# Column sums of a LayerNorm on VectorE, and part of the weights' low parts by accumulating DMA transfers

## The chip, the core and the metric

One core of one Trainium2 chip. The metric is the device time of one execution, in microseconds (us); lower is better. A core has TensorE (matrix products, its results go to PSUM), VectorE, ScalarE, GpSimd (POOL) and SyncE (SP). In this kernel SP's queue issues the loads, POOL's queue the transfers that add to what is already in the on-chip memory (SBUF).

## The reference, cut to what matters

One encoder layer on 256 positions with 2048 channels, in float32. The part that bears on the change:

```python
z = jnp.einsum("bsd,de->bse", x, w_in[i]) + b_in[i]          # 2048 -> 3072
y_conv = conformer_conv(z[..., :s1], z[..., s1:s2], ...)     # 1024 channels
y_pool = multiscale_pool(z[..., s2:s3], ...)                 # 512 channels
y_four = fourier_mix(z[..., s3:], ...)                       # 512 channels
mixed = jnp.concatenate([y_conv, y_pool, y_four], axis=-1)
mix_out = jnp.einsum("bsm,md->bsd", mixed, w_out[i]) + b_out[i]
x = layer_norm(ALPHA * x + mix_out, ln1_g[i], ln1_b[i])

def conformer_conv(val, gate, w_dw, b_dw, ln_g, ln_b):
    u = val * jax.nn.sigmoid(gate)
    y = depthwise_conv(u, w_dw, width=31) + b_dw
    return jax.nn.silu(layer_norm(y, ln_g, ln_b))            # mean and variance over 1024 channels
```

After it come a gated feed-forward part, a per-layer embedding part and a second LayerNorm.

## The kernel before, in words

**Products in three passes.** Every large product of float32 numbers is made of three matmuls in a rounded format (float32r): each operand is split into a high part (the rounded number) and a low part (the rest), and `mm3` (lines 162 to 165) adds high times high, high times low and low times high into one PSUM tile. `split` (line 123) makes the two parts: ScalarE writes the high part by a cast (line 125), VectorE the low part by a subtraction (line 126).

**Weights.** `weights` (line 128) walks over a weight matrix in blocks of four rows of 128: a load of 1 MB on SP's queue into one of four `raw` buffers (line 121), then for each half of the block (two rows of 128, 1024 columns) a split into one `whi` and one `wlo` tile; there are four buffers of each. `pump` then issues some of the convolution's work that is pending. `project` (line 167) runs the matmuls of one 512-column block: for each of 16 rows of weights two position halves of three matmuls, so 12 matmuls for each half block. All instructions are written in program order and a planner then orders them for each engine by its own estimate of what is ready, earlier program order first; each engine and each queue works strictly in that planned order.

**The stage around the change.** The input projection runs in six column blocks: `glu(0)`, `glu(1)`, the pool block (column 4), `glu(2)`, `glu(3)`, the Fourier block (column 5). Each `glu` gives two of the eight 128-channel blocks of the convolution, whose 31 taps are shared between VectorE and ScalarE (`convolve`, lines 281 to 291); channels lie on partitions, so `mixc` is 128 partitions x 8 blocks x 256 positions. Between `glu(2)` and `glu(3)` the residual is loaded (line 379), scaled by ScalarE (line 381), and its bias is added by two accumulating transfers of 1 MB on POOL's queue (line 382). POOL's queue also carries the small bias rows (line 205). Then the output projection starts with the rows that belong to the pool and Fourier halves (`out_chunk`, line 427; its sums are added to the residual in line 431): two column chunks before the convolution's LayerNorm and two after it, in program order.

**The convolution's LayerNorm.** Channels lie on partitions and blocks, so the sum over channels of a position goes across partitions. `channel_mean` (line 444) does it by TensorE: for each of eight blocks and two position halves a matmul with the block as the stationary operand and one column of ones (of 1/1024) as the moving one, in plain float32 (line 449). `across` (line 454) brings the result back to all partitions: a diagonal matrix with the values (line 459), multiplied by ones (line 460). `column` (line 463) copies the mean's column out of PSUM. `squares` subtracts the mean (line 472) and squares on ScalarE (line 474). The reciprocal root (`rsqrt`, lines 68 to 85) is made by VectorE on one column per position half. Then each block is multiplied by it (line 480), goes through the swish on ScalarE (line 482) and is split. These parts feed the rest of the output projection (line 494).

Later stages use the same `split` and `mm3`. In the feed-forward part POOL's queue carries accumulating transfers of 1 MB (lines 617 and 629).

Of the kernel before, what the change touches and what calls it, by code (L numbers as in the profile page):

```python
# [9 lines left out]
F32 = mybir.dt.float32  # L10
F32R = mybir.dt.float32r
I32 = mybir.dt.int32
AF = mybir.ActivationFunctionType
ALU = mybir.AluOpType
PSUM = bass.MemoryType.PSUM

P = 128
D = 2048
S = 256
NT = S // P  # L20
# [4 lines left out]
NC = 512  # L25
ALPHA = float(2.0 ** 0.25)
EPS = 1e-5
KD = D // P
NCH = 8
POOL_WINDOWS = (2, 4, 8, 16)  # L30

PUMP = 1.3
# [35 lines left out]
def rsqrt(nc, pool, var, shape, tag):  # L68

    v = pool.tile(shape, F32, name="rs_v", tag=tag + "v")  # L70
    nc.vector.tensor_scalar(v, var, EPS, None, op0=ALU.add)
    y = pool.tile(shape, F32, name="rs_y", tag=tag + "y")
    nc.vector.tensor_scalar(
        y.bitcast(I32), v.bitcast(I32), -0.5, float(0x5F3759DF), op0=ALU.mult, op1=ALU.add
    )
    nc.vector.tensor_scalar(v, v, -0.5, None, op0=ALU.mult)
    a = pool.tile(shape, F32, name="rs_a", tag=tag + "a")
    for _ in range(3):
        if shape[1] == 1:
            nc.vector.tensor_scalar(a, y, v, y, op0=ALU.mult, op1=ALU.mult)  # L80
        else:
            nc.vector.tensor_tensor(a, y, y, op=ALU.mult)
            nc.vector.tensor_tensor(a, a, v, op=ALU.mult)
        last = nc.vector.scalar_tensor_tensor(y, in0=a, scalar=1.5, in1=y, op0=ALU.add, op1=ALU.mult)  # L84
    return y, last
# [3 lines left out]
def encoder_layer(ctx: ExitStack, tc, t):  # L89
    nc = tc.nc  # L90
# [7 lines left out]
    ptp = ctx.enter_context(tc.tile_pool(name="ptp", bufs=2, space=PSUM))  # L98

    ident = cpool.tile([P, P], F32, name="ident")  # L100
# [4 lines left out]
    def pump(budget):  # L105

        if hold[0] > 0:
            hold[0] -= 1
            return
        credit[0] += budget  # L110
        while pending and credit[0] > 0:
            cost = next(pending[0], None)
            if cost is None:
                pending.pop(0)
            else:
                credit[0] -= cost
        if not pending:
            credit[0] = 0.0
# [6 lines left out]
        nc.scalar.copy(hi, src)  # L125
        return nc.vector.tensor_tensor(lo, src, hi.bitcast(F32), op=ALU.subtract)  # L126

    def weights(dram, nk, spare=0, first=False):

        for u in range(0, nk, 4):
            n = min(4, nk - u)
            raw = wraw.tile([P, n * NC], F32, name="raw", tag="raw")
            small_steps = first and u == 0
            if not small_steps:
                m = n // 2 if first and u == 4 else n
                for h in range(0, n, m):
                    load(raw[:, h * NC : (h + m) * NC], dram[u // 4][:, h * NC : (h + m) * NC])  # L140
            if u >= nk - spare:
                th = apool.tile([P, 8, S], F32R, name="ahi", tag="ahi").rearrange("p a b -> p (a b)")
                tl = apool.tile([P, 8, S], F32R, name="alo", tag="alo").rearrange("p a b -> p (a b)")
            for h in range(0, n, 2):
                if u >= nk - spare:
                    hi, lo = (
                        x[:, h * NC : (h + 2) * NC].rearrange("p (k n) -> p k n", n=NC) for x in (th, tl)
                    )
                else:
                    hi = wsp.tile([P, 2, NC], F32R, name="whi", tag="whi")  # L150
                    lo = wsp.tile([P, 2, NC], F32R, name="wlo", tag="wlo")
                src = raw[:, h * NC : (h + 2) * NC].rearrange("p (k n) -> p k n", n=NC)
                if not small_steps:
                    split(src, hi, lo)
                    pump(PUMP)
                for k in range(2):
                    if small_steps:
                        load(src[:, k, :], dram[0][:, (h + k) * NC : (h + k + 1) * NC])
                        split(src[:, k, :], hi[:, k, :], lo[:, k, :])
                    yield u + h + k, hi[:, k, :], lo[:, k, :]  # L160
# [3 lines left out]
        nc.tensor.matmul(out, ahi, wlo, start=False, stop=False, **more)  # L164
        nc.tensor.matmul(out, alo, whi, start=False, stop=stop, **more)  # L165

    def project(dram, nk, act, bias=None, behind=0, spare=0, first=False, halves=False):

        ps = [pacc.tile([P, NC], F32, name="acc", tag="acc") for _ in range(NT)]
        if halves:
            ps.append(pacc.tile([P, NC], F32, name="acc", tag="acc"))

        def step(i, k, hi, lo, whi, wlo):
            c = slice(P, S) if i else slice(0, P)
            n = slice((i - 1) * S, i * S) if halves and i else slice(0, NC)
            mm3(  # L180
                ps[i][:, : n.stop - n.start], hi[:, c], lo[:, c], whi[:, n], wlo[:, n],
                k == 0, k == nk - 1 and bias is None,
            )

        late = []
        ahead = act(0)
        for k, whi, wlo in weights(dram, nk, spare, first):
            if k == LAG:
                while deferred:
                    deferred.pop(0)()  # L190
            ops = (k, *(act(k) if k else ahead), whi, wlo)
            step(0, *ops)
            if k >= nk - behind:
                late.append(ops)
            else:
                for i in range(1, len(ps)):
                    step(i, *ops)
        for i in range(1, len(ps)):
            for ops in late:
                step(i, *ops)  # L200
        if bias is not None:
            one2, bsh, bsl, pool = bias[0]
            brow = pool.tile([2, NC], F32R, name="brow", tag="brow", bufs=2)
            for i, part in enumerate((bsh, bsl)):
                nc.gpsimd.dma_start(
                    brow[i : i + 1, :].rearrange("o (a b) -> o a b", b=P), part[4 * bias[1] : 4 * bias[1] + 4, :]
                )
            for j in range(NT):
                nc.tensor.matmul(ps[j], one2, brow, start=False, stop=True)
        return ps  # L210
# [20 lines left out]
    with tc.tile_pool(name="conv", bufs=1) as conv:  # L231
        par = conv.tile([P, C_END], F32, name="par")
        col = lambda c: par[:, c : c + 1]
        ones = conv.tile([P, P], F32, name="ones")
        mixc = conv.tile([P, 8, S], F32, name="mixc")
# [15 lines left out]
        xhi, xlo, xact = act_tiles(2)  # L251
# [12 lines left out]
        y = [mixc[:, i, :] for i in range(NCH)]  # L264
# [28 lines left out]

        def glu(c, act):

            ps = project(t["w_in"][c], KD, act, first=c == 0)
            if c == 0:
                nc.sync.dma_start(ident, t["const"][:, K_ID : K_ID + P])
                nc.sync.dma_start(par, t["par"])
                nc.sync.dma_start(ones, t["const"][:, K_ONE : K_ONE + P])  # L300
            deferred.append(lambda: glu_end(c, ps))
            if c == 0:
                hold[0] = HOLD
# [37 lines left out]
        mix = [pfp.tile([P, 4, S], F32, name=f"mix{i}", tag="mix") for i in range(2)]  # L341


        ps = project(t["w_in"][4], KD, xact, bias=(biases, 4))
        with tc.issue_after(last_load[0].ins):
            nc.sync.dma_start(kst[:, K_MT - K_CH :], t["const"][:, K_MT:])

# [38 lines left out]
        glu(3, xact)  # L386


        ps = project(t["w_in"][5], KD, xact, bias=(biases, 5))

        def fourier_end(ps):
            zf = pfp.tile([P, NC], F32, name="zpf", tag="zpf", bufs=3)
# [50 lines left out]

        def channel_mean(src):

            out = [ptp.tile([P, NC], F32, name="tp", tag="tp")[:, 0:1] for _ in range(NT)]
            for i, x in enumerate(src):
                for j in range(NT):
                    nc.tensor.matmul(
                        out[j], x[:, j * P : (j + 1) * P], ones[:, 0:1], start=i == 0, stop=i == NCH - 1  # L450
                    )
            return out

        def across(v):

            out = ptp.tile([P, NC], F32, name="tp", tag="tp")
            for j in range(NT):
                diag = plep.tile([P, P], F32, name="diag", tag="diag", bufs=2)
                nc.vector.tensor_scalar(diag, ident, v[j], float(NCH * P), op0=ALU.mult, op1=ALU.mult)
                nc.tensor.matmul(out[:, j * P : (j + 1) * P], ones, diag, start=True, stop=True)  # L460
            return out[:, :S]

        def column(src):
            out = plep.tile([P, 1], F32, name="colv", tag="colv", bufs=4)
            nc.vector.tensor_copy(out, src)
            return out

        mean = across([column(m) for m in channel_mean(y)])

        def squares():  # L470
            for i in range(NCH):
                nc.vector.tensor_tensor(y[i], y[i], mean, op=ALU.subtract)
                sq = plep.tile([P, S], F32, name="sq", tag="sq", bufs=4)
                nc.scalar.activation(sq, y[i], AF.Square)
                yield sq

        rstd = across([rsqrt(nc, plep, v, [P, 1], f"cv{j}")[0] for j, v in enumerate(channel_mean(squares()))])
        chi, clo, cact = act_tiles(1)
        for i in range(NCH):
            nc.vector.tensor_tensor(y[i], y[i], rstd, op=ALU.mult)  # L480
# [331 lines left out]
```

## Time and profile before

| | |
|---|---|
| median of 3 runs | 1098.87 us (1097.17 to 1099.01) |
| the profiled execution | 1097.18 us |
| its span, first to last instruction | 1095.4 us |
| TensorE (PE) busy | 1069.1 us, 98% |
| TensorE weight loads (PEld) | 870.7 us, 79% |
| VectorE (DVE) busy | 811.6 us, 74% |
| ScalarE (ACT) busy | 618.0 us, 56% |
| GpSimd (POOL) busy | 22.2 us, 2% |
| mean granted TensorE clock | 0.993 |

How to read it: the share of an engine is a mean over stages with different limits. Matmuls overlap their neighbours, so the distance between their starts says more than the duration of one. A line such as `acc<-wlo,ahi` names the tile written and the tiles read. "idle before" is the time in which an engine stood still just before an instruction, and what ended it. The time of an execution is a little more than its span.

### The profile page before, as it was taken

How to read it: one execution, taken by the hardware profiler on the slowest of the kernel's cores; microseconds unless marked ns; L12 is line 12 of the kernel's file. 1: busy time of each engine (PE TensorE's matmuls, PEld its weight loads, DVE VectorE, ACT ScalarE, POOL GpSimd, SP SyncE). 2: the span in 40 equal slices, each digit the busy share in tenths (PEclk: the TensorE clock that was granted, in tenths of full speed). 3: DMA queues.
4: the chain of work that ended last, by engine and by line, in shares of the span. 5: the costliest groups of instructions: out<-in, count | busy, mean ns of one | idle time of the engine just before them, and what ended most of it. 6: DMA issues, size and time to landing. Idle time of an engine off the chain costs nothing.

```text
span 1095.4 us, 12577 instructions
## 1 busy us (share of the span) xinstructions
PE 1069.1 (98%) x4768; PEld 870.7 (79%) x4768; DVE 811.6 (74%) x972; ACT 618.0 (56%) x795; POOL 22.2 (2%) x46
## 2 busy tenths in 40 slices
PE   8999999999799999999999999999999999999995
PEld 6888878886588888888888888888888878888884
DVE  5899998877955557878744578788755567887676
ACT  5888875647554446656533366566543355665440
POOL 0000000000000000000000000000000000000000
PEclk9999999999899999999999999999999999999998
DMA  9777543644455676678655766786755567867532
GB/s 352 281 283 209 187 172 130 227 154 173 154 192 189 252 236 228 217 260 250 250 188 183 221 223 221 243 282 224 255 211 182 197 197 240 290 217 268 189 116 77
DMA packets 35361, 236.15 MB, mean 216 GB/s; under 512 B 4028, under 2 KB 4580, under 8 KB 7780
## 3 DMA queue, kind: packets, MB, share of 16 engines
q1 hardware_dynamic: 32004, 212.27, 51.7%
q0 software_dynamic: 3296, 23.08, 11.4%
q8 instruction: 37, 0.61, 0.2%
q14 instruction: 24, 0.20, 0.1%
HBM read 233.23 MB, written 2.10 MB: 215 GB/s over the span
## 4 chain that ended last, share of the span: by engine, by line
PE 71%; DVE 2%; ACT 0%; issue 0%; DVEq 0%; ACTq 0%
PE acc L164 24%; PE acc L163 23%; PE acc L165 23%; PE tp L672 1%; DVE res L705 0%; DVE res L710 0%; DVE sraw L627 0%; ACT whi L125 0%; DVE wlo L126 0%; DVE st L701 0%; DVE res L700 0%; DVE rs_a L80 0%; DVE rs_y L84 0%; DVE mv L225 0%; DVEq L808 0%
## 5 line engine op out<-in xcount | busy, mean ns | idle before, releaser
L126 DVE TENSOR_TENSOR wlo<-raw,whi 128x1024 fp32r<-128x1024 f32 (+1 forms) x336 | 405.2, 1215 | 189.4 <-ACT whi L125 184.3
L125 ACT CAST whi<-raw 128x1024 fp32r<-128x1024 f32 (+1 forms) x336 | 351.0, 1047 | 304.7 <-PE acc L165 293.2
L163 PE MATMUL acc<-whi,ahi 128*128 128x512 f32 x1112 | 438.5, 396 | 11.8 <-ACT whi L125 11.8
L164 PE MATMUL acc<-wlo,ahi 128*128 128x512 f32 x1112 | 437.0, 393 | 0.3 <-DVE wlo L126 0.3
L165 PE MATMUL acc<-whi,alo 128*128 128x512 f32 x1112 | 433.9, 392 | 0.0
L163 PEld LDWEIGHTS acc<-whi,ahi 128*128 128x128 f32 x1112 | 209.8, 189 | 59.0 <-ACT whi L125 12.8
L164 PEld LDWEIGHTS acc<-wlo,ahi 128*128 128x128 f32 x1112 | 210.0, 189 | 46.8 <-DVE wlo L126 4.5
L165 PEld LDWEIGHTS acc<-whi,alo 128*128 128x128 f32 x1112 | 209.7, 189 | 43.8
L126 DVE TENSOR_TENSOR wlo<-sraw,whi 128x1024 fp32r<-128x1024 f32 x100 | 119.8, 1221 | 45.3 <-ACT whi L125 45.3
L125 ACT CAST whi<-sraw 128x1024 fp32r<-128x1024 f32 x100 | 104.5, 1054 | 84.4 <-PE acc L165 59.2
L163 PE MATMUL acc<-whi,hhi 128*128 128x512 f32 x328 | 129.9, 396 | 0.0
L164 PE MATMUL acc<-wlo,hhi 128*128 128x512 f32 x328 | 129.6, 395 | 0.0
L165 PE MATMUL acc<-whi,hlo 128*128 128x512 f32 x328 | 129.6, 395 | 0.0
L165 PEld LDWEIGHTS acc<-whi,hlo 128*128 128x128 f32 x328 | 61.6, 188 | 15.0
L163 PEld LDWEIGHTS acc<-whi,hhi 128*128 128x128 f32 x328 | 61.6, 188 | 14.8
L164 PEld LDWEIGHTS acc<-wlo,hhi 128*128 128x128 f32 x328 | 61.6, 188 | 14.7
L281 ACT ACTIVATE pr<-uT,par 128x256 f32<-128x256 f32 x128 | 56.8, 501 | 5.6 <-DVE part L283 5.4
L287 DVE SCALAR_TENSOR_TENSOR mixc<-uT,par,mixc 128x256 f32<-128x256 f32 x104 | 46.3, 472 | 0.0
L283 DVE TENSOR_TENSOR part<-part,pr 128x512 f32<-128x512 f32 x64 | 43.4, 678 | 0.3 <-ACT pr L281 0.2
L616 DVE TENSOR_TENSOR sraw<-raw,sraw 128x2048 f32<-128x2048 f32 x10 | 22.9, 2292 | 2.4 <-DMA raw<-in_w_gate 2.2
L627 DVE TENSOR_TENSOR sraw<-sraw 128x2048 f32<-128x2048 f32 x10 | 22.9, 2287 | 0.1
L617 POOL DMA_DIRECT2D sraw<-in_w_up x10 | 8.6, 861 | 688.7 <-DVE sraw L616 516.5
(130 smaller groups left out, 511.8 us busy)
## 6 DMA issues: line engine op xcount, KB each, us to landing
raw<-in_w_gate SPq DMA_DIRECT2D x44, 1024.0 KB, 5.7
raw<-in_w_down SPq DMA_DIRECT2D x44, 1024.0 KB, 4.8
raw<-in_w_up SPq DMA_DIRECT2D x24, 1024.0 KB, 4.9
raw<-in_w_in SPq DMA_DIRECT2D x22, 1024.0 KB, 5.0
sraw<-in_w_up SPq DMA_DIRECT2D x20, 1024.0 KB, 7.6
raw<-in_w_out SPq DMA_DIRECT2D x16, 1024.0 KB, 4.8
raw<-in_w_pg SPq DMA_DIRECT2D x16, 1024.0 KB, 4.9
sraw<-in_w_up POOLq DMA_DIRECT2D x10, 1024.0 KB, 9.3
```

The lines of the kernel that those rows point to most:

```text
L125: nc.scalar.copy(hi, src)
L126: return nc.vector.tensor_tensor(lo, src, hi.bitcast(F32), op=ALU.subtract)
L163: nc.tensor.matmul(out, ahi, whi, start=start, stop=False, **more)
L164: nc.tensor.matmul(out, ahi, wlo, start=False, stop=False, **more)
L165: nc.tensor.matmul(out, alo, whi, start=False, stop=stop, **more)
L281: nc.scalar.mul(pr[:, n, :], uT[ch][:, k : k + S], w)
L283: nc.vector.tensor_tensor(part, part, pr, op=ALU.add)
L287: nc.vector.scalar_tensor_tensor(y[ch], in0=uT[ch][:, k : k + S], scalar=w, in1=y[ch], op0=ALU.mult, op1=ALU.add)
L616: nc.vector.tensor_tensor(tsum, b11, b12, op=ALU.add)
L617: nc.gpsimd.dma_start(b12, up[1], accum_op=ALU.add)
L627: nc.vector.tensor_tensor(tsum, tsum, b22, op=ALU.add)
L672: nc.tensor.transpose(tp[:, i * P : (i + 1) * P], g[:, i * P : (i + 1) * P], ident)
```

## The change

The LayerNorm's sums over the eight channel blocks are made by VectorE additions (1024, 512, 256 columns), and one plain float32 matmul with a 128 x 128 matrix of ones sums across partitions and spreads the result to all of them. The reciprocal root is taken on all 256 positions on all partitions. The squares are made two blocks at a time.

In five of the six input projections (all but the first), the third of the four weight blocks (`u == 8`) is split differently: ScalarE writes the high part and then the negated rounded weights into the low tile; a transfer of 512 KB on POOL's queue adds the raw weights to it.

```diff
-    def weights(dram, nk, spare=0, first=False):
+    def weights(dram, nk, spare=0, first=False, added=None):
...
-                if not small_steps:
+                if u == added:
+                    nc.scalar.copy(hi, src)
+                    nc.scalar.mul(lo, src, -1.0)
+                    nc.gpsimd.dma_start(lo.bitcast(F32), src, accum_op=ALU.add)
+                    pump(PUMP)
+                elif not small_steps:
                     split(src, hi, lo)
                     pump(PUMP)
...
-            ps = project(t["w_in"][c], KD, act, first=c == 0)
+            ps = project(t["w_in"][c], KD, act, first=c == 0, added=8 if c else None)
...
-        ps = project(t["w_in"][4], KD, xact, bias=(biases, 4))
+        ps = project(t["w_in"][4], KD, xact, bias=(biases, 4), added=8)
...
-        ps = project(t["w_in"][5], KD, xact, bias=(biases, 5))
+        ps = project(t["w_in"][5], KD, xact, bias=(biases, 5), added=8)
...
         def channel_mean(src):
-            out = [ptp.tile([P, NC], F32, name="tp", tag="tp")[:, 0:1] for _ in range(NT)]
-            for i, x in enumerate(src):
-                for j in range(NT):
-                    nc.tensor.matmul(
-                        out[j], x[:, j * P : (j + 1) * P], ones[:, 0:1], start=i == 0, stop=i == NCH - 1
-                    )
+            a4 = plep.tile([P, D], F32, name="a4", tag="ple1").rearrange("p (n s) -> p n s", s=S)
+            nc.vector.tensor_tensor(a4[:, 0:4, :], src[:, 0:4, :], src[:, 4:8, :], op=ALU.add)
+            for n in (2, 1):
+                nc.vector.tensor_tensor(a4[:, 0:n, :], a4[:, 0:n, :], a4[:, n : 2 * n, :], op=ALU.add)
+            out = ptp.tile([P, NC], F32, name="tp", tag="tp")[:, :S]
+            nc.tensor.matmul(out, ones, a4[:, 0, :], start=True, stop=True)
             return out
...
-        mean = across([column(m) for m in channel_mean(y)])
...
-        rstd = across([rsqrt(nc, plep, v, [P, 1], f"cv{j}")[0] for j, v in enumerate(channel_mean(squares()))])
+        mean = channel_mean(mixc)
+        sq = plep.tile([P, D], F32, name="sq", tag="ple0").rearrange("p (n s) -> p n s", s=S)
+        for i in range(0, NCH, 2):
+            for n in (i, i + 1):
+                nc.vector.tensor_tensor(y[n], y[n], mean, op=ALU.subtract)
+            nc.scalar.activation(sq[:, i : i + 2, :], mixc[:, i : i + 2, :], AF.Square)
+        rstd = rsqrt(nc, plep, channel_mean(sq), [P, S], "cv")[0]
```

The functions `across`, `column` and `squares` are removed.

## Rows read from the trace of the kernel before

**Rows 1.** Windows view: busy us of PE, PEld, DVE, ACT, POOL; clock; DMA share; GB/s.
```profile
60.00:170.00 110.00, 110.00 (x489) 89.18 (x488) 109.56 (x184) 92.23 (x171) 1.77 (x2) 1.00 0.61 208
```

**Rows 2.** Timeline of TensorE near 171 us: start, us, engine, line, operation.
```profile
170.64 2.73 PE L449 MATMUL tp<-ones,mixc 128*128 128x1 f32 x24
173.24 0.48 PE L163 MATMUL acc<-whi,ahi 128*128 128x512 f32 x1
173.55 0.39 PE L164 MATMUL acc<-wlo,ahi 128*128 128x512 f32 x1
173.78 0.40 PE L163 MATMUL acc<-whi,ahi 128*128 128x512 f32 x1
```

**Rows 3.** Timeline of VectorE, 171 to 213 us.
```profile
171.07 1.23 DVE L126 TENSOR_TENSOR alo<-mix,ahi 128x1024 fp32r<-128x1024 f32 x1
...
185.41 0.68 DVE L291 TENSOR_TENSOR mixc<-mixc,part 128x512 f32<-128x512 f32 x1
...
211.24 0.69 DVE L431 TENSOR_TENSOR res<-acc,res 128x512 f32<-128x512 f32 x1 [0.29 <-PE acc L165]
211.85 0.75 DVE L126 TENSOR_TENSOR alo<-m,ahi 128x256 fp32r<-128x256 f32 x2
```

**Rows 4.** Instructions of lines 449 and 460: ns min/median/max, first and last start.
```profile
L449 PE MATMUL tp<-ones,mixc x32: 164/250/251, 170.6 to 187.0; 128*128 128x1 f32 x32
...
L449 PE MATMUL tp<-ones,sq x32: 164/250/271, 192.7 to 199.7; 128*128 128x1 f32 x32
...
L460 PE MATMUL tp<-diag,ones x8: 270/274/275, 190.0 to 207.5; 128*128 128x128 f32 x8
```

**Rows 5.** Timeline of TensorE in the pool map.
```profile
83.66 0.59 PE L364 MATMUL tp<-pd,par 128*128 128x256 f32 x2
84.09 1.03 PE L358 MATMUL tp<-kst,zpf 128*128 128x256 f32 x4
```

**Rows 6.** Groups of VectorE by line, 150 to 212 us.
```profile
L126 DVE TENSOR_TENSOR wlo<-raw,whi 128x1024 fp32r<-128x1024 f32 x15 | 18.2, 1218 | 0.1
...
L283 DVE TENSOR_TENSOR part<-part,pr 128x512 f32<-128x512 f32 x16 | 10.9, 679 | 0.0
...
L472 DVE TENSOR_TENSOR mixc<-mixc,tp 128x256 f32<-128x256 f32 x8 | 2.7, 413 | 0.5 <-PE tp L460 0.5
...
L80 DVE TENSOR_SCALAR rs_a<-rs_y,rs_v 128x1 f32<-128x1 f32 x6 | 1.4, 269 | 0.0
...
L71 DVE TENSOR_SCALAR rs_v<-tp 128x1 f32<-128x1 f32 x2 | 0.3, 159 | 4.2 <-PE tp L449 4.1
```

**Rows 7.** Timeline of ScalarE, 29 to 105 us.
```profile
30.06 1.26 ACT L309 COPY z<-acc 128x512 f32<-128x512 f32 x2 [2.50 <-PE acc L165]
...
35.27 1.04 ACT L125 CAST whi<-raw 128x1024 fp32r<-128x1024 f32 x1
...
38.61 1.04 ACT L125 CAST whi<-raw 128x1024 fp32r<-128x1024 f32 x1
...
86.08 1.05 ACT L125 CAST whi<-raw 128x1024 fp32r<-128x1024 f32 x1
...
103.59 1.27 ACT L309 COPY z<-acc 128x512 f32<-128x512 f32 x2 [0.98 <-PE acc L165]
```

**Rows 8.** DMA issues: KB each, median us to landing; last, all landings of line 629.
```profile
sraw<-in_w_gate POOLq DMA_DIRECT2D x10, 1024.0 KB, 8.7
...
raw<-in_w_ple SPq DMA_DIRECT2D x4, 512.0 KB, 3.6
...
brow<-bsh POOLq DMA_DIRECT2D x2, 2.0 KB, 2.1
...
DMA to landing us min/median/max: 8.0/8.7/8.8
```

**Rows 9.** POOL's second accumulation on the residual, and its landing.
```profile
85.25 0.87 POOL L382 DMA_DIRECT2D res<-in_brow  x1 [1.44 <-ACT res L381]
...
DMA to landing us min/median/max: 13.8/13.8/13.8
```

More of the change, by code (lines that the diff above doesn't have):

```diff
@@ L165, in mm3, with project @@
         nc.tensor.matmul(out, alo, whi, start=False, stop=stop, **more)
-    def project(dram, nk, act, bias=None, behind=0, spare=0, first=False, halves=False):
+    def project(dram, nk, act, bias=None, behind=0, spare=0, first=False, halves=False, added=None):
         ps = [pacc.tile([P, NC], F32, name="acc", tag="acc") for _ in range(NT)]
@@ L186, in project @@
         ahead = act(0)
-        for k, whi, wlo in weights(dram, nk, spare, first):
+        for k, whi, wlo in weights(dram, nk, spare, first, added):
             if k == LAG:
@@ L444, in channel_mean @@
         def channel_mean(src):
-            out = [ptp.tile([P, NC], F32, name="tp", tag="tp")[:, 0:1] for _ in range(NT)]
-            for i, x in enumerate(src):
-                for j in range(NT):
-                    nc.tensor.matmul(
-                        out[j], x[:, j * P : (j + 1) * P], ones[:, 0:1], start=i == 0, stop=i == NCH - 1
-                    )
-            return out
[L454 to L466, printed above, removed]
-        mean = across([column(m) for m in channel_mean(y)])
[L470 to L475, printed above, removed]
```

## The prediction

> **What bounds the kernel now.** I read the busy time of the stretches first. From 60 to 170 us (the input projections) TensorE is busy 110.00 of 110 us, VectorE 109.56, ScalarE 92.23 [rows 1]. A full row of VectorE does not say that it bounds: what decides is whether TensorE's matmuls are ever late. In the timeline consecutive 512-column matmuls start 0.23 us apart [rows 2], in this stretch and nearly everywhere else, so **TensorE's own work sets the end**, and VectorE runs just ahead of it. A microsecond off VectorE gains nothing by itself; one off TensorE is gained if nothing else becomes late. The second view is the chain of the LayerNorm: the first low part of the activation is written at 211.85 us, when TensorE has just ended the last of the early output chunks (VectorE's addition of that chunk waited for TensorE until 211.24) [rows 3]. There is almost no slack, so everything that lengthens that chain counts.
>
> **TensorE's part of the LayerNorm.** Removed: 64 passes with one column (the 32 column-sum matmuls appear as two passes each) and the 8 passes of the diagonal matmuls [rows 4]. 24 of them in a row take 2.73 us, 0.114 each [rows 2], so 72 x 0.114 = 8.2 us. Added: two matmuls of 256 columns in plain float. Such a pair of passes holds up the next start by 0.43 us in the pool map [rows 5], 0.5 with the step back, so 1.0 us. Net **-7.2 us**; bounds -7.7 and -6.5, as the small passes sit singly or in rows.
>
> **A cover that goes.** The row of 24 passes stands where TensorE would otherwise wait for the split of the Fourier half: its low part starts at 171.07 us, so the high part came just before [rows 2, 3]. TensorE would have been ready at 170.64. The high part allows the first matmuls, so **+0.45 us**; none if VectorE's relief brings it earlier, 1.6 if the low part is wanted at once.
>
> **VectorE's part of the LayerNorm.** The sums of eight channel blocks are additions of 1024, 512 and 256 columns: by the nearest rows 1.22 + 0.68 + 0.41, less some 0.07 of overlap each, 2.1 us, twice 4.2 [rows 6]. The reciprocal root over 256 columns instead of one has 12 operations; 256-column ones cost 2.7/8 = 0.34 us in a row [rows 6], so 4.1. Only the largest group of what goes, the 1.4 us of the column products, I credit [rows 6]; the rest is small. So at most +6.9 us on VectorE between the end of the convolution and the first low part. Against it, two subtractions in each of five projections go: 10 x 1.14 (1.22 less the overlap) = -11.4 us [rows 6], all before 146 us, where VectorE is full. Net at the first low part VectorE is 4.5 us ahead of before, TensorE 6.75 ahead. But before, VectorE stood 4.1 us waiting for the column sums of the squares [rows 6], a wait on work that now shrinks. The eight squares become four wide ones on ScalarE, half idle there. I take **+0.5 us** of waiting; ends 0 and 4.4 (the fourth rival). The subtractions and products by mean and root stay as they are.
>
> **The accumulating transfers.** In each of five projections, at the third block of four, ScalarE makes the high part (1.04 us), then the negated copy (the same, so 10 x 1.05 = 10.5 us, ScalarE from 84% to some 92% of the stretch [rows 1, 7]), then POOL issues a 512 KB transfer that adds the raw weights, twice per projection. Nothing follows on VectorE for these tiles. The price of such a transfer from on-chip memory is in no row. Bounds: 3.6 us for a plain 512 KB load on SP's queue, 8.0 for the quickest accumulating 1 MB on POOL's [rows 8]. Between them: 2.1 us for a transfer of 2 KB and 8.7 for 1 MB give 2.1 + 6.6/2 = 5.4 us [rows 8]; I take **5.4**, since these rows are of the same queue.
> How much may it take? There are four buffers. When TensorE frees one, the tile put into it is wanted three half-blocks later, 3 x 12 x 0.227 + 0.23 = 8.4 us; cast and copy take 2.1 and the hand-overs 0.2, so **6.1 us** are left. 5.4 fits, if ScalarE casts at once. It does not always:
> - The second projection: the first ended at 29.9 (the copy that waited for it is at 30.06) [rows 7]; 96 matmuls and 0.9 us of transposes later this one ends at 52.6, so its two tiles' low parts are wanted at 41.95 and 44.65. Casts stood at 35.27 and 38.61 [rows 7]. First: 37.35 + 5.4 = 42.75. Second, pushed by the first copy: 41.75 + 5.4 = 47.15, 2.5 us late in all. TensorE can take high-part matmuls first, as it does at 173.78 [rows 2], which needs the order to be planned so; I take half, **1.25**, ends 0 and 2.5.
> - The third column block (from 76 us): it ends at 103.4 [rows 7], so the second tile is wanted at 95.5. It is cast at 86.08 + 1.05 and ready to issue at 89.2. POOL's queue is in order, and the residual's accumulation was issued at 85.25 and took 13.8 us, to 99.05 [rows 7, 9]. The raw block stays occupied until our transfer ends, so the next 1 MB load, which competed then, is held back; by that the queue frees near 97, and the tile lands some 3.3 us later, at 100.3 at most, against 95.5 and the 2.5 us that TensorE is late by then: 2 late, I take **0.8**, ends 0 and 4.5.
> - The other three have margins from 0 to 2 us; nothing, ends 0 and 1.9 each (8.0 less 6.1).
> The held raw blocks delay SP's next load by some 7 us; the loads come about 15 us ahead of use, so no term.
>
> By the Trainium skill, DMA: Bandwidth & Descriptors, section "Anatomy of one DMA — SWDGE (gpsimd) path", a transfer on this queue takes 2.0 us and its bytes at 436 GB/s: an estimate of 3.2 us here, by which no tile would be late and the sum would be -6.3. By the same formula 1 MB takes 4.4, while this trace shows 8.0 to 8.8 for the accumulating ones [rows 8]; I let the trace decide.
>
> **The sum:** -7.2 + 0.45 + 0.5 + 1.25 + 0.8 = -4.2 us. The profiled execution took 1097.18 us (span 1095.4 and 1.8 around it), so 1093.0; the median shown, 1098.87, lies 1.7 above it. I predict **1094.6** for the median.
>
> **Rivals.**
> 1. Nothing is late: the transfers take under 6.1 us everywhere and the plan brings the rest. -7.2 + 0.45 = -6.75: 1092.1. For it: 3.6 us for 512 KB on SP's queue. Against it: ScalarE's lag in the second projection. Chance 0.2.
> 2. The transfers are short enough by themselves, but the one behind the residual's accumulation in POOL's queue is late in full (99.05 + 3.3 = 102.3, 4.5 late), and the second projection's too (2.5). -7.2 + 0.45 + 0.5 + 2.5 + 4.5 = +0.75: 1099.6. For it: the second of the two accumulations landed 13.8 us after its issue. The Trainium skill, DMA: Bandwidth & Descriptors, section "SWDGE vs HWDGE vs iDMA", says that only one software queue is allocated; no run here shows more than one either. Chance 0.17.
> 3. **Slower:** an accumulating 512 KB transfer costs nearly what 1 MB does, 8.0 us. Then each projection is late by 8.0 - 6.1 = 1.9 us once (its second tile shifts with the first): five times 9.5, so -7.2 + 0.45 + 9.5 + 0.5 = +3.25: 1102.1. The place is TensorE's first low-part matmul of the third block; it decides from 7.5 us per transfer on, where 5 x 1.4 eats the gain. For it: transfers of 2 KB already take 2.1 us, and reading, adding and writing back may cost the same per row whatever its length. Against it: the larger part of 8.7 us grows with bytes by the two rows. Chance 0.16.
> 4. The LayerNorm's chain on VectorE decides: VectorE's relief is lost because the last convolution steps stand behind additions that wait for TensorE. Then the convolution ends with TensorE's chunk at 186.0 - 2.3 = 183.7 [rows 3] and VectorE has 4.2 + 2.7 + 4.1 + 2.7 us of LayerNorm, some eight weight splits of 1.14 and 3.5 of other work and waits: 26.3, to 210.0, where TensorE wants it at 205.6. 4.4 late: -7.2 + 0.45 + 4.4 + 2 = -0.35: 1098.5. Chance 0.1.
>
> **How the numbers follow.** My forecast (some tiles late by about a microsecond) has 0.37, with its own range from 1092.5 to 1097. 0.2% is 2.2 us, about what a measurement of this kernel can tell from no change: the borders are 1096.7 and 1101.1. Faster: the forecast and rival 1, 0.57. Within: rival 2 and most of rival 4, with the forecast's upper edge against their lower ones, 0.22. Slower: rival 3 and the upper ends of rivals 2 and 4, 0.21. The range goes from 1091.5 (rival 1 with the larger gain on TensorE) to 1102.0 (rival 3 nearly whole).
>
> **What would show it.** Right: the one-column and diagonal passes are gone and four 256-column passes stand in their place; starts 0.23 us apart through the added blocks, except short waits in the second and third column blocks; POOL shows ten 512 KB transfers landing in 5 to 6 us; VectorE no longer full from 60 to 170 us; first low part of the normalised activation near 205 us. Wrong: idle TensorE before low-part matmuls in every added block (rival 3); a landing of over 12 us near 90 us (rival 2); a TensorE gap of 3 us or more near 205 us with VectorE full (rival 4). The prediction falls if an accumulating transfer takes over 7.5 us, or if the order on the queues is replanned so that other work is late.

## The result, and the profile after

The changed kernel took **1104.03 us** in the median (1103.38 to 1104.26), the kernel before 1098.57 on the same chip: ratio 1.0051, interval 1.0034 to 1.0068. It is slower by 5.5 us where the prediction had it 4 us faster. The profiled execution took 1103.38 us, its span is 1101.6, 6.2 more than before.

The first view is again the stretch of the input projections. This is the window that answers to [rows 1] (busy us of PE, PEld, DVE, ACT, POOL; clock; DMA share; GB/s), of the kernel after:

```profile
60.00:170.00 110.00, 105.00 (x457) 84.96 (x455) 97.15 (x169) 93.91 (x173) 8.65 (x10) 0.97 0.79 243
```

VectorE got its relief: 97.15 us where it had been full. But TensorE, full before, is idle for 5 us, and its clock is below 1. The view of TensorE's waits up to 300 us says for what (us in total, times, longest):

```profile
PE acc L170 <- DMA wlo<-raw: 6.8, 2, 5.0
PE acc L169 <- ACT ahi L125: 1.6, 2, 1.1
```

Neither group is in the same view of the kernel before. Line 170 is the matmul of low weights (line 164 before), 169 and 171 the other two passes, 155 the cast in the added blocks, 156 the negated copy, 157 the transfer, 388 the residual's accumulation, 387 its scaling; in the experiments these numbers shift by some lines. TensorE's timeline has the two waits for a transfer, first in the second projection, then in the third column block:

```profile
41.78 0.62 PE L169 MATMUL acc<-whi,ahi 128*128 128x512 f32 x2
44.21 0.50 PE L170 MATMUL acc<-wlo,ahi 128*128 128x512 f32 x1 [1.81 <-DMA wlo<-raw]
44.55 0.39 PE L171 MATMUL acc<-whi,alo 128*128 128x512 f32 x1
44.78 0.51 PE L170 MATMUL acc<-wlo,ahi 128*128 128x512 f32 x1
45.08 0.63 PE L171 MATMUL acc<-whi,alo 128*128 128x512 f32 x1
45.51 0.63 PE L169 MATMUL acc<-whi,ahi 128*128 128x512 f32 x1
...
48.42 0.39 PE L170 MATMUL acc<-wlo,ahi 128*128 128x512 f32 x1
...
98.93 0.39 PE L169 MATMUL acc<-whi,ahi 128*128 128x512 f32 x1
104.32 0.79 PE L170 MATMUL acc<-wlo,ahi 128*128 128x512 f32 x1 [5.00 <-DMA wlo<-raw]
104.91 0.63 PE L171 MATMUL acc<-whi,alo 128*128 128x512 f32 x1
105.34 0.63 PE L169 MATMUL acc<-whi,ahi 128*128 128x512 f32 x1
...
109.91 0.40 PE L171 MATMUL acc<-whi,alo 128*128 128x512 f32 x1
```

Read it by the starts, 0.23 us apart when nothing is late. From 41.78 two matmuls take 0.45, and the next starts 2.43 after 41.78: 1.98 lost. From 98.93 to 104.32 the loss is 5.16. And it does not stop there: behind each wait the starts come to stand 0.43 apart, from 45.08 on in the second projection and from 104.91 on in the third column block. From 44.21 to 48.42 are 11 starts, 2.5 us at the usual distance, so 1.7 more are lost; from 104.32 to 109.91 are 13, so 2.6 more. The windows show the granted clock (the column behind POOL):

```profile
42.00:44.00 2.00, 0.39 (x2) 0.00 (x0) 2.00 (x4) 2.00 (x4) 0.20 (x1) 1.00 1.04 190
46.00:48.00 2.00, 2.00 (x6) 1.59 (x5) 0.60 (x2) 0.00 (x0) 1.84 (x4) 0.50 0.23 40
98.00:100.00 2.00, 1.32 (x6) 0.75 (x4) 1.90 (x3) 2.00 (x5) 0.00 (x0) 1.00 0.98 205
102.00:104.00 2.00, 0.00 (x0) 0.00 (x0) 1.34 (x3) 0.00 (x0) 0.00 (x0) 0.73 0.56 109
106.00:108.00 2.00, 2.00 (x6) 1.52 (x6) 0.00 (x0) 0.00 (x0) 0.00 (x0) 0.50 0.87 360
```

Both times it fell to 0.50, the lower level of 1.2 GHz. In the third column block it fell while TensorE stood still (0.73 in the mean from 102 to 104), and stayed there when TensorE was busy again; in the second projection it fell only after TensorE had started again, near 45 us. Behind the two waits 4.3 us were lost in all. The Trainium skill, TensorE: Matmul & The Clock Gate, section "HAM oscillation — how this bites in real kernels", describes that a wait for a DMA can lower the clock so that the work behind it starts slow. The trace agrees for the third column block.

Why the tile was late is on POOL's timeline:

```profile
84.06 0.85 POOL L157 DMA_DIRECT2D wlo<-raw  x1 [19.11 <-ACT wlo L156]
86.37 0.86 POOL L388 DMA_DIRECT2D res<-in_brow  x1 [1.46 <-DMA raw<-in_w_in]
88.72 0.86 POOL L388 DMA_DIRECT2D res<-in_brow  x1 [1.48 <-ACT pd L368]
90.33 0.86 POOL L157 DMA_DIRECT2D wlo<-raw  x1 [0.75 <-DVE mix L373]
```

The view of line 157 around the last of them, with its landing:

```profile
L157 POOL DMA_DIRECT2D wlo<-raw x1: 860/860/860, 90.3 to 90.3; - x1
...
DMA to landing us min/median/max: 13.9/13.9/13.9
```

The second accumulation of 1 MB, issued at 85.25 before [rows 9], goes out at 88.72; it lands 13.1 us later, at 101.8. Our 512 KB behind it land at 90.33 + 13.9 = 104.2, and TensorE goes on at 104.32. POOL was idle for 1.48 us ahead of that accumulation, so the block's first transfer, which stands ahead in the queue, did not hold up its issue. The accumulation has to follow the scaling of the residual on ScalarE, and the last part of that scaling ends 3.5 us later than before (first line before, second after; the issue follows its end by 0.3 us in both):

```profile
83.28 1.67 ACT L381 ACTIVATE res<-res 128x512 f32<-128x512 f32 x3
86.23 2.19 ACT L387 ACTIVATE res<-res 128x512 f32<-128x512 f32 x4
```

Most of this is the time lost in the second projection. The first accumulation goes out at 86.37 here, at 85.74 in the run below with the transfers alone (2.7 us lost in the second projection instead of 3.7), at 83.25 in the run below with the low part first everywhere (0.67 lost), and at 82.91 before; in all three runs the block's first transfer stands ahead of it.

Last, the LayerNorm's end. ScalarE's timeline:

```profile
213.56 1.06 ACT L125 CAST whi<-raw 128x1024 fp32r<-128x1024 f32 x1 [1.66 <-PE acc L171]
214.64 1.28 ACT L471 ACT_TABLE_LOAD   x1
215.93 1.09 ACT L471 ACTIVATE m<-mixc,par 128x256 f32<-128x256 f32 x2
216.93 0.70 ACT L125 CAST ahi<-m 128x256 fp32r<-128x256 f32 x2
```

and TensorE's first matmul with the normalised activation, which had waited for that cast:

```profile
217.37 0.50 PE L169 MATMUL acc<-whi,ahi 128*128 128x512 f32 x1 [1.12 <-ACT ahi L125]
```

TensorE loses 1.28 us there, and 0.63 at the split of the Fourier half (182.32). **The account:** 1.98 + 1.7 + 5.16 + 2.6 + 0.63 + 1.28 = 13.35 us lost, and the span grew by 6.2, so 7.15 were gained. What is left over in this sum is put down to the small passes, whose gain was forecast at 7.2.

### The profile page after: what moved, and what is told of

Same layout as the page of the kernel before. It is cut to its first block, busy times and chain, and to the rows that moved or that the text cites. A ratio compares the mean times of both kernels' runs of the same rounds, so it can differ in the third digit from the quotient of the medians.

```text
span 1101.6 us, 12452 instructions
## 1 busy us (share of the span) xinstructions
PE 1067.3 (97%) x4700; PEld 866.0 (79%) x4700; DVE 806.9 (73%) x956; ACT 625.0 (57%) x801; POOL 30.9 (3%) x56
## 3 DMA queue, kind: packets, MB, share of 16 engines
q0 software_dynamic: 4736, 28.32, 13.8%
## 4 chain that ended last, share of the span: by engine, by line
PE 71%; DVE 2%; ACT 0%; issue 0%; DVEq 0%; ACTq 0%
PE acc L170 23%; PE acc L169 23%; PE acc L171 23%; PE tp L661 1%; DVE res L694 0%; DVE res L699 0%; DVE sraw L616 0%; ACT whi L125 0%; DVE wlo L126 0%; DVE st L690 0%; DVE res L689 0%; DVE rs_a L80 0%; DVE rs_y L84 0%; DVE mv L231 0%; DVEq L797 0%
## 5 line engine op out<-in xcount | busy, mean ns | idle before, releaser
L126 DVE TENSOR_TENSOR wlo<-raw,whi 128x1024 fp32r<-128x1024 f32 (+1 forms) x326 | 393.8, 1217 | 206.4 <-ACT whi L125 201.7
L125 ACT CAST whi<-raw 128x1024 fp32r<-128x1024 f32 (+1 forms) x326 | 340.4, 1047 | 311.2 <-PE acc L171 302.7
L169 PE MATMUL acc<-whi,ahi 128*128 128x512 f32 x1112 | 439.9, 397 | 13.4 <-ACT whi L125 11.8
```

The lines of the kernel that those rows point to most:

```text
L169: nc.tensor.matmul(out, ahi, whi, start=start, stop=False, **more)
```

## The experiments

Each ratio is against the kernel before on the same chip, whose medians lay between 1098.02 and 1098.50 us beside these runs.

**Each half alone.** First the new LayerNorm without the transfers: `added=None` in all projections.

> The LayerNorm's sums on VectorE alone, no accumulating weight transfers. Theory A (the loss comes from late transfers; the sums by themselves gain): TensorE loses 7.2 us of small passes, keeps about 2 to 4 us of waiting near the end of the LayerNorm because VectorE is not relieved: 1093 to 1096 us, ratio to before 0.995 to 0.998. Theory B (the sums on VectorE cost what they save, the transfers only add to it): 1098 us or more, with a TensorE gap of 5 us or more near 205 us.

Measured: **1101.35 us**, ratio 1.0027 (1.0018 to 1.0036). Theory B's gap was there, larger than thought, in TensorE's timeline:

```profile
204.45 0.39 PE L165 MATMUL acc<-whi,alo 128*128 128x512 f32 x1
213.06 0.79 PE L163 MATMUL acc<-whi,ahi 128*128 128x512 f32 x1 [8.22 <-ACT ahi L125]
```

and the windows ahead of the gap and around its end:

```profile
190.00:200.00 10.00, 10.00 (x46) 8.24 (x45) 10.00 (x18) 6.30 (x8) 0.00 (x0) 1.00 0.84 336
206.00:216.00 10.00, 2.90 (x6) 1.89 (x7) 8.71 (x21) 4.65 (x9) 0.00 (x0) 0.56 0.40 149
```

VectorE, the third busy time of the row, is full for 10 of 10 us, and still busy for 8.71 from 206 to 216. So the LayerNorm's sums alone give up the 7.2 us and more: 8.4 lost in the gap, and 2.3 more behind it at a lower clock, which had fallen in the gap (0.56 in the mean from 206 to 216 us). Then the transfers without the new LayerNorm (the old functions put back).

> The accumulating transfers alone, with the old LayerNorm. Theory A: the two waits (2.0 and 5.2 us) and the half clock after them (1.6 and 2.9 us) stay, nothing is gained: 11.7 us, 1110 us, ratio 1.0105. Theory B: the transfers cost less than the sums: under 1104 us.

Measured: **1109.15 us**, 1.0097 (1.0083 to 1.0112), with both waits for the transfers as in the changed kernel (1.98 and 5.17 us). Behind the first of them the clock stayed at 1.00 here, and a second wait of 0.71 us came for the projection's next tile. Alone the halves cost 3 and 11 us, together 5.5: the transfers' relief of VectorE turns the gap of 8.4 us into one of 1.28. The halves belong together, and the loss is in the transfers.

**The third column block.** Without its two transfers:

```diff
-            ps = project(t["w_in"][c], KD, act, first=c == 0, added=8 if c else None)
+            ps = project(t["w_in"][c], KD, act, first=c == 0, added=8 if c in (1, 3) else None)
```

> The whole change, but no accumulating transfers in the third column block, the one that shares POOL's queue with the residual's accumulations. Theory A: the wait of 5.2 us and 2.9 us of half clock go: 1104.0 - 8.1 = 1096 us; the first wait of 2.0 us stays. Rival (all the transfers are slow when loads compete): other blocks wait as well, 1100 us or more.

Measured: **1095.75 us**, 0.9976 (0.9966 to 0.9985). That block cost 8 us. The second projection's wait is still there, 1.92 us and then 0.65, at a clock of 1.00. But is it the transfers, or their place on POOL's queue? Here the transfers stay and only POOL's order changes; the planned order of every other engine is the same:

```diff
-                    nc.gpsimd.dma_start(lo.bitcast(F32), src, accum_op=ALU.add)
+                    last_add[0] = nc.gpsimd.dma_start(lo.bitcast(F32), src, accum_op=ALU.add)
...
-                nc.gpsimd.dma_start(
-                    res[j], t["brow"][0:16, :].rearrange("a b -> (a b)").partition_broadcast(P), accum_op=ALU.add
-                )
+                with tc.issue_after(last_add[0].ins):
+                    row = t["brow"][0:16, :].rearrange("a b -> (a b)").partition_broadcast(P)
+                    nc.gpsimd.dma_start(res[j], row, accum_op=ALU.add)
```

> The whole change; only on POOL's queue the two accumulations on the residual stand behind the third block's second weight transfer. Every other engine's order is the same. Theory A (the transfer was late because it stood behind 2 MB of accumulation in one queue): it lands in 5 to 8 us instead of 13.9, the wait of 5.2 us and its half clock go, 1096 us. Rival (the transfer was slow by the competing loads, not by its place): it still lands after 10 us or more, 1102 us or more.

Measured: **1096.08 us**, 0.9981 (0.9972 to 0.9989). POOL's timeline:

```profile
84.29 0.85 POOL L157 DMA_DIRECT2D wlo<-raw  x1 [19.14 <-DVE mixc L293]
90.53 0.85 POOL L157 DMA_DIRECT2D wlo<-raw  x1 [5.39 <-ACT wlo L156]
91.11 2.06 POOL L390 DMA_DIRECT2D res<-in_brow  x2
```

and the landing of the transfer at 90.53, from the view of line 157:

```profile
DMA to landing us min/median/max: 4.9/4.9/4.9
```

The transfer goes out 0.2 us later than in the changed kernel and lands 9 us faster, although the two accumulations, issued 0.6 us behind it, are under way beside it; TensorE doesn't wait in this block at all. **The queue place alone made the 8 us** (5.16 of waiting, 2.6 of clock).

**The second projection.** In the changed kernel ScalarE's timeline shows why that tile is late:

```profile
34.72 1.05 ACT L155 CAST whi<-raw 128x1024 fp32r<-128x1024 f32 x1
35.66 0.91 ACT L287 ACTIVATE part<-uT,par 128x256 f32<-128x256 f32 x2
36.47 1.70 ACT L287 ACTIVATE pr<-uT,par 128x256 f32<-128x256 f32 x4
38.07 1.05 ACT L156 ACTIVATE wlo<-raw 128x1024 fp32r<-128x1024 f32 x1
```

The plan put the convolution's products between the cast and the negated copy, so the transfer was issued at 39.44. The next run adds to the last one that the low part goes first:

```diff
-                    nc.scalar.copy(hi, src)
                     nc.scalar.mul(lo, src, -1.0)
                     last_add[0] = nc.gpsimd.dma_start(lo.bitcast(F32), src, accum_op=ALU.add)
+                    nc.scalar.copy(hi, src)
```

> The run with the residual's accumulations behind the third column block's transfers (1096.08 us) with one more edit: the negated copy and the transfer are issued ahead of the high-part cast. Theory A: the second projection's wait of 2.0 us on the low weights comes from ScalarE, whose planned order puts convolution products between cast and copy; with the copy first the transfer is issued some 2 us earlier, the wait falls to 1 us or less, the half clock behind it (about 1.6 us) goes too: 1092.5 to 1094.5 us. Theory B: the planner moves the products in front of the new pair as well, or the high part is now late instead: a wait of about 2 us stays at the same place, 1095.5 to 1097.

Measured: **1094.84 us**, 0.9972 (0.9962 to 0.9981). The transfer is issued at 35.85, the wait is 0.67 us, and the clock stays at 1.00: theory A, but just outside its range, since another wait came up, in the fifth projection. TensorE's timeline there:

```profile
115.95 0.39 PE L169 MATMUL acc<-whi,ahi 128*128 128x512 f32 x1
118.84 0.50 PE L170 MATMUL acc<-wlo,ahi 128*128 128x512 f32 x1 [2.50 <-DMA wlo<-raw]
```

and the windows around it:

```profile
112.00:116.00 4.00, 4.00 (x20) 3.26 (x18) 4.00 (x8) 4.00 (x9) 0.87 (x1) 1.00 1.01 247
118.00:120.00 2.00, 1.16 (x5) 0.97 (x6) 2.00 (x4) 0.97 (x3) 0.00 (x0) 1.00 0.35 68
```

The two transfers there took 10.6 and 9.2 us (8.0 and 6.7 in the changed kernel), with the DMA engines fully busy (1.01 from 112 to 116). The moved accumulations lead to this, I think: the second one ends near 105.6 us and the loads it competed with come later. That was not tried by itself. All four kernels with the accumulations moved wait there (0.46, 2.66, 1.87 and 1.96 us); of the others only one by more than 0.3 us (0.34).

Two runs leave out the transfers of the second projection, one with the cast first and one with the low part first.

> The run with the residual's accumulations behind the third column block's transfers (1096.08 us) without the two transfers of the second projection; four column blocks keep theirs. Theory A: that wait cost 2.0 us and the half clock behind it 1.6, so 1092.5 to 1094. Theory B: VectorE loses 2.3 us of its relief, and the LayerNorm's wait near 216 us (0.65 + 1.28) grows by as much, which eats the gain: 1095 to 1096.5.

> Both edits: copy and transfer ahead of the cast, and no transfers in the second projection. If the order on ScalarE also made the short wait in the third column block (0.46 us) that goes too, and the result is 0 to 1 us below the run without transfers in the second projection (1092 to 1094); if the order matters in the second projection alone, the two runs are within 0.5 us of each other.

Measured: **1094.44** (0.9967, 0.9955 to 0.9979) and **1094.43** (0.9965, 0.9952 to 0.9977). The LayerNorm's waits stayed at 0.65 and 1.28 (a shorter one ahead of the sums' matmul grew from 0.27 to 0.58 in the first), so theory B of the first is out; but both have the wait in the fifth projection too (1.87 and 1.96), which theory A's range and the second expectation had not counted: the 0.46 us that the latter puts in the third column block stand at 119 us, in the fifth projection, and did not go. The order on ScalarE matters in the second projection alone, as far as these two tell.

**The residual left where it was, low part first everywhere:**

> The changed kernel with the residual's accumulations where they were, ahead on POOL's queue, and the negated copy and transfer ahead of the cast. Theory A: the third column block's wait of 5.2 us is made by the queue (2 MB ahead), so it stays at 4 us or more with its half clock although the transfer is issued earlier; only the second projection's wait goes: 1100 to 1101.5 us, with a landing of 12 us or more. Theory B: it is ScalarE's lag there too: the wait falls under 2 us, 1095 to 1097.

Measured: **1093.87 us**, 0.9959 (0.9946 to 0.9972). Theory A's number missed by 6 us, and theory B's by one. POOL's timeline shows that A's premise had gone:

```profile
80.99 0.85 POOL L156 DMA_DIRECT2D wlo<-raw  x1 [19.06 <-ACT wlo L155]
83.25 0.86 POOL L388 DMA_DIRECT2D res<-in_brow  x1 [1.40 <-ACT res L387]
86.08 0.85 POOL L156 DMA_DIRECT2D wlo<-raw  x1 [1.97 <-ACT wlo L155]
86.70 1.12 POOL L388 DMA_DIRECT2D res<-in_brow  x1
```

and the landing of the transfer at 86.08:

```profile
DMA to landing us min/median/max: 11.1/11.1/11.1
```

With everything earlier, the plan put the second transfer ahead of the second accumulation: one MB ahead of it instead of two, issued 4.2 us sooner, landed at 97.2, and a wait of 0.93 us. Two more runs were to separate ScalarE's order in this block from that in the others; in the first the third column block keeps the cast first, in the second it alone has the low part first.

> The changed kernel with the negated copy and the transfer ahead of the cast in four column blocks; the third column block keeps cast, copy, transfer. The run with copy and transfer first everywhere (1093.87 us) had moved the second transfer of the third column block ahead of the second residual accumulation on POOL's queue. Theory A: the third block's own order on ScalarE decides what stands ahead of that transfer, but here, too, POOL's order is planned with one accumulation ahead of it and one behind (as the blocks before run earlier), so a landing of about 11 us and a wait of 1 to 3 us: 1095 to 1098. Theory B: the transfer is issued near 90 us again and lands near 104: the wait of 5 us and its half clock return, 1100 to 1101.5.

> The changed kernel with copy and transfer ahead of the cast in the third column block alone; there both residual accumulations still stand ahead of the second transfer on POOL's queue. Theory A (the queue makes the wait): the transfer is made ready some 3 us earlier but lands behind 2 MB, 13 us or more after issue; a wait of 3 us or more stays at about 99 us: 1100 to 1103, with the second projection's 2.0 us and its half clock as they were. Theory B (ScalarE's lag makes it): the wait falls under 2 us: 1095 to 1097.5.

Measured: **1094.17** (0.9967, 0.9955 to 0.9980) and **1103.72** (1.0048, 1.0035 to 1.0060). The first has one accumulation ahead, as its theory A has it, a landing of 11.1 us and a wait of 0.91, and is quicker than that theory's range; the second has two ahead, 14.0 us and 5.25, as its theory A has it, 0.7 above its range. In both ScalarE really has the copy first in this block, as the changed kernel has (82.73 the copy, 83.98 the cast): the plan had turned the pair round by itself, so the written order there does nothing. The two runs are in effect the run with the low part first everywhere and the changed kernel once more, and their theories on this block's own order on ScalarE were not put to the test. What the other blocks' order does is to shift the plan, and with it POOL's queue. Over all eleven kernels with these transfers the wait goes with what stands ahead (the shorter root and the moved cast are told below):

| 1 MB accumulations ahead | issue to landing, us | TensorE's wait, us |
|---|---|---|
| 2 (changed kernel; low part first in this block alone; transfers alone) | 13.9; 14.0; 13.9 | 5.16; 5.25; 5.17 |
| 1 (low part first everywhere; all but this block; shorter root; moved cast) | 11.1; 11.1; 10.3; 10.5 | 0.93; 0.91; none; 0.33 |
| 0 (residual behind; the same, low part first; the two without the second projection's) | 4.9; 5.4; 6.5; 6.4 | none |

The middle row was also issued 4 us earlier than the upper, so its small wait is not the queue's doing alone. But the first runs of the upper and the lower row differ in the queue at nearly equal times of issue (90.33 and 90.53), and so do the first of the middle row and the second of the lower (86.08 and 85.96).

**The LayerNorm's wait.** Two runs on the kernel with the low part first everywhere.

> The run with copy and transfer first everywhere (1093.87 us), with two of the reciprocal root's three refining steps (one left out, so its output is a little less exact): three VectorE operations of 0.42 us fewer. With that the plan puts ScalarE's table load and the first swish one weight cast earlier. Theory A: the wait of 1.29 us near 207 us stands behind that chain (root, cast that waits for TensorE, table load 1.28, swish, cast); it falls to 0.3 us or less: 1092.3 to 1093. Theory B: another work decides and the wait stays: 1093.5 to 1094.3.

> The run with copy and transfer first everywhere (1093.87 us), all of the computation, with one weight cast of the output projection put behind the first two swishes on ScalarE (it stood ahead of the table load and waited for TensorE to free its buffer); VectorE's root keeps its three steps. Theory A: ScalarE's order alone makes the wait of 1.29 us near 207 us, so it falls to about 0.3 us (the root ends at 204.7, then product, swish and cast): 1092.5 to 1093.2. Theory B: the length of VectorE's chain makes it, as the shorter root took it away: the wait stays at 1 us or more, 1093.6 to 1094.3.

Measured: **1092.43** (0.9950, 0.9937 to 0.9964) for the shorter root, and its wait is gone (so is the 0.93 us of the third column block, at the same order on POOL's queue, with a landing of 10.3 us instead of 11.1); **1093.27** (0.9952, 0.9940 to 0.9964) for the moved cast. In the second, TensorE starts its high parts on time, and then its timeline has:

```profile
206.99 0.39 PE L178 MATMUL acc<-whi,ahi 128*128 128x512 f32 x1
208.27 0.50 PE L180 MATMUL acc<-whi,alo 128*128 128x512 f32 x1 [0.89 <-DVE alo L128]
```

The wait went from ScalarE's high part to VectorE's low part, 1.05 us instead of 1.29; the gain of 0.6 us is too small to be told from none. So neither theory holds as put: the cast and the table load end the wait, but VectorE's chain is late by nearly as much behind them. Of the versions that compute all, the low part first everywhere and this one are the quickest, 4.6 and 5.2 us below the kernel before, and some 10 below the changed kernel.

## Why the prediction was wrong, point by point

- **TensorE's 7.2 us: right.** The account of the span leaves 7.15 for it. With the low part first everywhere the span fell by 3.0 and the waits sum to 3.5, which leaves 6.5. Taken over the stretch alone, from ScalarE's copy behind the Fourier projection (150.62 us before, 161.64 after) to the first transpose behind the output projection (255.81 and 261.70), 5.1 us were gained in spite of 1.9 of waiting: 7.0.
- **The third column block failed, a term of 0.8 that measured 7.8.** The prediction saw that the tile stands behind the residual's accumulation, and then took 2 us off for a load that would be held back, so that the queue would be free near 97. Its own working came to 2 us of lateness, of which it took 0.8 without a reason. The queue was free at 101.8. Of these 4.8 us, 1.3 are relief that did not come: the accumulation took 13.1 us instead of 13.8, where the prediction had some 11.8. The other 3.5 are its later issue: the prediction kept it at 85.25, but the time lost in the second projection had moved the scaling, and the accumulation with it, to 88.72. The terms were added as if one did not move the other. The wait of 5.16 lies just outside the stated ends of 0 and 4.5.
- **The clock was left out.** 4.3 us were lost behind the two waits, at a granted clock of 0.50. No term, no bound and no rival had it. It is most of what lies between the second rival (the right place, 1099.6 us) and the measured 1104.
- **The second projection: 1.25 was taken, half of 2.5; 1.98 and 1.7 of clock came.** The halving failed: where the clock stayed at 1.00, the projection's two tiles cost 1.98 + 0.71 and 1.92 + 0.65 us, so nearly the whole 2.5. "If ScalarE casts at once" was weighed for the time of the casts, but not that the plan can put products between the two halves of the new pair. Low part first made the wait 0.67.
- **512 KB at 5.4 us: right for most of those with nothing long ahead of them.** Landings took 4.6 to 6.1 us in the second projection and the pool block, and 4.9 in the third block's second transfer with the residual behind; but 7.9 for the third block's first transfer, which had the queue to itself, and 5.1 to 8.0 in the last two. The estimate of 3.2 us from the Trainium skill (DMA: Bandwidth & Descriptors, "Anatomy of one DMA — SWDGE (gpsimd) path") is under every one of the ten landings in the changed kernel; the measurement decides. The third rival (each block late) didn't come: the pool block, the fifth and the sixth projection show no wait in the changed kernel. Two landings, the 7.9 and an 8.0 in the fifth projection, were over the 7.5 us that the prediction named as its limit, and no wait stands behind them, so the 6.1 us that the prediction allowed were too few there.
- **The LayerNorm's chain: 0.95 forecast with the lost cover, 1.9 measured.** The relief by the transfers, on which this term rested, is real: without it the gap is 8.4 us, nearly twice the fourth rival's 4.4. Two chains end late there by nearly the same. One is ScalarE's, which the prediction did not have: a table load of 1.28 us behind a cast that waits for TensorE. The other is VectorE's: with the cast moved away its low part still came 1.05 us late.

The range ended at 1102.0 us. The slower side had its chance mainly for a wrong reason, a transfer that is long everywhere (rival 3). The queue was named beside it, as the upper end of rival 2; the lower clock was not.

## What to carry to other kernels

When a change adds DMAs to a queue that is worked in order, write down the whole queue around each of them, with what each entry itself waits for, and carry time lost earlier through to the landings: 2 MB ahead turned 4.9 us into 13.9. A wait of TensorE should be priced with the clock that may come behind it, which in the changed kernel added half as much again to a wait of 5 us and nearly doubled one of 2, and in other runs added nothing to one of 2. And when one half of a change frees the engine that the other half loads, time the halves alone, since each by itself may look worse than nothing.

## What the runs showed of the hardware that was not expected

Waits of TensorE are not alike for the clock. After the 5.16 and 1.98 us of the changed kernel it fell to 0.50 (2.4 to 1.2 GHz), but after the 2.66 us wait in the fifth projection, and the 1.87 and 1.96 of the two runs beside it, it stayed at 1.00. Even the wait in the second projection differs, at the same place and of the same length, in one profiled execution of each kernel: after 1.98, 1.99 (residual behind) and 1.94 us (low part first in the third block alone) the clock fell, after 1.98 (transfers alone) and 1.92 us (no transfers in the third block) it did not. These lines are from the last of them:

```profile
45.22 0.50 PE L170 MATMUL acc<-wlo,ahi 128*128 128x512 f32 x1 [1.76 <-DMA wlo<-raw]
...
48.50 0.50 PE L170 MATMUL acc<-wlo,ahi 128*128 128x512 f32 x1 [0.49 <-DMA wlo<-raw]
```

```profile
46.00:48.00 2.00, 2.00 (x9) 1.32 (x7) 1.66 (x3) 0.74 (x3) 1.10 (x3) 1.00 0.75 140
```

There the next tile made a second wait of 0.65 us. The changed kernel has no such wait, since TensorE was slower by then, so an estimate of the clock's own price is about 1 of the 1.7 us lost behind its first wait. TensorE was full ahead of all these waits; what tells them apart was not tried.
